# A planned DeltaNet stage: two transposing copies of each block inverse moved to the end of their slot, three large table writes spread over six slots, and one slot more ahead of the weight scales

## The chip, the cores and the metric

The kernel runs on one core of a Trainium2 chip. The metric is the device time of one launch in microseconds (us). TensorE is called PE here, VectorE DVE, ScalarE ACT, GpSimd POOL; SP is the SyncE queue, which in this kernel does nothing but issue DMAs.

## The reference

One encoder layer is computed for two sequences, of 2048 and 1024 tokens, with a model width of 1024. All projections of the normalised input come from one matrix `w_in`; two token mixers run on parts of it, a neighbourhood attention with a relative position bias and a bidirectional gated DeltaNet:

```python
h = _rms_norm(x, norm_g)
proj = jnp.einsum('btd,de->bte', h, w_in)
...
bias = rpb[:, dr_idx[None, None, :, None], dc_idx[:, :, None, :]]
s = jnp.where(col_ok[:, :, None, :], s + bias.astype(jnp.float32), -jnp.inf)
...
a_mat = jnp.where(strict, jnp.einsum('bhnid,bhnjd->bhnij', kb, k) * decay, 0.0) + jnp.eye(CHUNK, dtype=q.dtype)
sol = lax.linalg.triangular_solve(a_mat, rhs, left_side=True, lower=True, unit_diagonal=True)
...
S, o = lax.scan(step, S0, xs)   # one scan per direction over chunks of 64 tokens
```

The two mixers' outputs are gated, projected, merged and put through one more product with a residual. The triangular solve is what the kernel calls an inverse; the masked bias is what its bias table holds.

## The kernel before

**Two stages and an end.** `deltanet()` (from L167) takes the first 1660 us or so: it makes the projections of the input, the DeltaNet operands, the inverses and the scans. From 1668 us on the neighbourhood attention runs (its products are the tile `ppn`), and the branch products, the merge and the output follow.

**The planner.** In `deltanet()` every instruction of every engine and of the SP queue is emitted from one loop, `step_slot()` (L226 to L248), and `Pinned.call` chains each engine's instructions in the order of emission (so every instruction of the trace has the line of that helper, L61). A step is called a slot. The work is written as Python generators; each `yield n` hands back and comes again n slots later. A slot has fixed points, and between them `fill` puts product matmuls on PE until a cost of a quarter, a half, three quarters and the whole of `UNITS` is reached:

```python
            launch()
            advance("S")
            fill(0.25 * UNITS)
            advance("I")
            fill(0.5 * UNITS)
            advance("WH")
            advance("O", MOST)
            fill(0.75 * UNITS)
            ... # what mid() listed, then what end() listed
            advance("F")
            fill(UNITS)
```

S are the scans (PE `pk`, ACT `vn`, DVE `t` and `S`), I the inverses, W and H the weights, the input's rows and side work such as the bias table, O the operands (DVE `P` and `Vt`, the convolution's taps, at 128x512 each), F the decay tables. `launch` opens new generators when their inputs are planned, and issues the loads of the half tiles `hh` and `hl`, the normalised input in two f16 parts, from `hdr` in DRAM. An operand generator goes ahead only while DVE and ACT have been given less than a cost of MOST in the slot. `end(f, ...)` puts a call at the slot's end, with every generator of the slot ahead of it on the engine's queue.

**The filler.** `products()` (L706) multiplies a tile `w` of `w_in` with a half tile: 24 f16 matmuls of 128x256 into the PSUM tile `pp`, which ACT then reads (into `raw`, the convolution's input, or with a tanh into `thz`, the gates), and for the gates `z` DVE multiplies `thz` by `pp` one slot later. Two half banks of a PSUM tile are handed out in turn, so a product begins only when an earlier `pp` has been read. Where the filler has no product whose weights and input are planned, PE gets f32 transposes of a constant called `idle`, up to half of the slot.

**An inverse** (`inverse`, L987). There are twelve, one per head and pair of blocks, never two at once. They work in three buffers that exist once: X, U (in the trace `YT`) and W (`Yo`). In its first slot four DMAs on SP load from `ed` (eight DMAs of the operands' `P` wrote it) two quarters of X and two of U. Two slots later ACT copies U's rows 32 to 63 into X with a transposed reading order, and DVE does the same for rows 96 to 127 (L1002 and L1003, `X<-YT` 32x1024). One slot after that DVE sets X's diagonal (MEMSET X) and POOL clears U (memset YT). A number of slots later the result goes out to `rd` in four DMAs, comes back as `RR` (which takes X's buffer) in the slot after, and two slots later DVE does a STREAM_TRANSPOSE on it.

**The weights** (`weights(k)`, L530, once for each half k of the rows). A weight tile is staged (`wst<-in_w_in`, 256 KB, issued at a slot's end), and DVE reduces it to its largest absolute value per row (`wm<-wst`). When both halves of a group's tiles have been reduced, `factors` (L396) makes the scales: DVE reduces `wm` to `wma`, one slot later PE spreads it over the partitions with transposes `pm`, and DVE reduces `pm` and makes `wsc` and `wfc`. `split_tile` then reads the staged weights again and makes their two f16 parts (`w`).

**The bias table** (`bias_table`, L495) is a side work in the middle of the stage. It fills the DRAM table `ud`, which the attention reads later in 256 loads `bt<-ud`: three large writes of a constant from `ng` over the whole table, one third each, and then 48 small ones `ud<-rp`, two to a slot.

Of the kernel before, what the change touches and what calls it, by code (L numbers as in the profile page):

```python
# [12 lines left out]
AF = mybir.ActivationFunctionType  # L13
# [32 lines left out]
def emit(nc, tc, x_prompt, x_sample, norm_g, w_in, attn_q_norm_g, attn_k_norm_g, attn_rpb, dn_conv_w, dn_a_log,  # L46
# [31 lines left out]
    V, S, G, T, SY = (Pinned(e) for e in (nc.vector, nc.scalar, nc.gpsimd, nc.tensor, nc.sync))  # L78
# [22 lines left out]
    def pow2(m, p, s, k, V=V):  # L101

        V.tensor_scalar_max(m, m, 1e-30)
        V.tensor_scalar(p.bitcast(I32), m.bitcast(I32), 0x7F800000, None, op0=ALU.bitwise_and)
        V.tensor_scalar(s.bitcast(I32), p.bitcast(I32), -1.0, float((254 + k) << 23), op0=MUL, op1=ADD)
# [7 lines left out]
    def allmax(sm, m2, m, ps):  # L113


        n = m.shape[1]
        for a in range(0, n, ps[2]):
            c = min(ps[2], n - a)
            pm = ps[0].tile([128, ps[2], 128], F32, name="pm", tag=ps[1])
            for i in range(c):  # L120
                T.transpose(pm[:, i], m[:, a + i:a + i + 1].to_broadcast([128, 128]), ident)
            V.tensor_reduce(m2[:, a:a + c], pm[:, 0:c], axis=AX.X, op=MAX)
# [44 lines left out]
    def deltanet():  # L167
# [26 lines left out]
        def end(f, *a):  # L194

            ends_.append((f, a))
# [199 lines left out]
        def factors(a, b, ts):  # L396

            n = b - a
            m3 = sm.tile([128, 3, 8], F32, name="wma", bufs=2)
            m, m2, p = (m3[:, i] for i in range(3))  # L400
            V.tensor_reduce(m[:, 0:n], wm2[:, a:b], axis=AX.X, op=MAX)
            yield
            pms = []
            for c in range(0, n, 4):
                pm = ps_tr.tile([128, 4, 128], F32, name="pm", tag="tr")
                for i in range(c, min(c + 4, n)):
                    T.transpose(pm[:, i - c], m[:, i:i + 1].to_broadcast([128, 128]), ident)
                pms.append(pm)
            if prologue:
                yield  # L410
            for c, pm in zip(range(0, n, 4), pms):
                k = min(4, n - c)
                V.tensor_reduce(m2[:, c:c + k], pm[:, 0:k], axis=AX.X, op=MAX)
            pow2(m2[:, 0:n], p[:, 0:n], wsc[:, a:b], 14)
            V.tensor_scalar(wfc[:, a:b], p[:, 0:n], pg, 2.0 ** -24, op0=MUL, op1=MUL)
            for t in ts:
                if t.kind == "z":
                    f = wfc[:, t.n:t.n + 1]
                    V.tensor_copy(zf[:, 4 * t.i + t.h:4 * t.i + t.h + 1], f)
                    if t.i == 0:  # L420
                        V.tensor_tensor(dngz[:, t.h:t.h + 1], dng, f, op=MUL)
# [73 lines left out]
        def bias_table():  # L495


            gq2, gk2 = sm.tile([128, 1], F32, name="gq2", bufs=1), sm.tile([128, 1], F32, name="gk2", bufs=1)
            for j in range(2):
                SY.dma_start(gq2[64 * j:64 * j + 64], attn_q_norm_g[0].rearrange("(p o) -> p o", o=1))  # L500
                SY.dma_start(gk2[64 * j:64 * j + 64], attn_k_norm_g[0].rearrange("(p o) -> p o", o=1))
            rp = wk.tile([120, 64], F32, name="rp", tag="gr", bufs=1)
            rp, ng = rp[:, 0:31], rp[:, 32:64]
            SY.dma_start(rp, attn_rpb[0].rearrange("h r c -> (h r) c"))
            G.memset(ng, NEG)
            yield 2

            V.scalar_tensor_tensor(gg, in0=gq2, scalar=0.125, in1=gk2, op0=MUL, op1=MUL)
            V.scalar_tensor_tensor(gq2, in0=gg, scalar=-1.0, in1=gg, op0=MUL, op1=MAX)
            yield  # L510
            allmax(sm, gk2, gq2, TR)
            V.tensor_scalar_max(gk2, gk2, 2.0 ** -10)
            pow2(gk2, pq, gq2, 0)
            V.tensor_tensor(gg, gg, gq2, op=MUL)
            V.tensor_scalar_mul(npq, pq, -1.0)
            V.tensor_scalar_mul(rp, rp, gq2[:120])
            for ct in range(3):
                SY.dma_start(ud[16 * ct:16 * ct + 16].rearrange("i r k -> r i k"), ng[:, None, :].to_broadcast([120, 16, 32]))
            yield 3
            for ct, off in enumerate((0, -8, -16)):  # L520
                for ci in range(16):
                    w0 = (max(ci - 8, 0), ci, min(8 + ci, 16))[ct]
                    d0 = w0 + off - ci + 15
                    SY.dma_start(ud[16 * ct + ci, :, w0:w0 + 16], rp[:, d0:d0 + 16])
                    if ci % 2:
                        yield
# [3 lines left out]
        def weights(k):  # L530

            def max_(*a):
                yield from maximum(*a, k)
                maxed[k] += 1

            extra = [v[0][:, 256 * i:256 * i + 256] for v in (w_branch_a, w_branch_b) for i in range(4)]
            extra += [w_out[0][:, 128 * i:128 * i + 128] for i in range(8)]
            extra += [win[:, c:c + 128] for c in (QA, KA, VA)]
            extra = list(enumerate(extra, NT + 1))
            for p in range(1, 5):  # L540
                ts = [s[p] for s in streams if len(s) > p]
                for t in ts:
                    yield from max_(win[:, t.c:t.c + 128], t.n)
                if k:
                    while maxed[0] < maxed[1]:
                        yield
                    yield from factors(ts[0].n, ts[-1].n + 1, ts)
                    facs[0] = p
                    yield
                while facs[0] < p:  # L550
                    yield
                for s in streams[:4]:
                    yield from split_tile(s[p], s[p - 1], k)
                if p < 4:
                    for s in streams[4:]:
                        for _ in range(2):
                            if extra:
                                i, src = extra.pop(0)
                                yield from max_(src, i)
                        yield from split_tile(s[p], s[p - 1], k)  # L560
                else:
                    for i, src in extra:
                        yield from max_(src, i)
            if not k:
                return
            while maxed[0] < maxed[1]:
                yield

            m1 = sm.tile([128, 2], F32, name="am1", bufs=1)
            V.tensor_reduce(m1[:, 0:1], wm2[:, NT + 1:NT + 9], axis=AX.XY, op=MAX)  # L570
            V.tensor_reduce(m1[:, 1:2], wm2[:, NT + 9:NT + 17], axis=AX.XY, op=MAX)
            m3 = sm.tile([128, 3], F32, name="am4", bufs=1)
            V.tensor_reduce(m3, wm2[:, NT + 17:NT + 20], axis=AX.X, op=MAX)
            yield
            m2 = sm.tile([128, 2], F32, name="am2", bufs=1)
            allmax(sm, m2, m1, TR)
            pow2(m2, abp[:, 0:2], abp[:, 2:4], 14)
            V.tensor_scalar_mul(so4, so_, 0.25)
            outs.append(1)
            yield  # L580
            m2 = sm.tile([128, 3], F32, name="am3", bufs=1)
            allmax(sm, m2, m3, TR)
            s3 = sm.tile([128, 3], F32, name="as3", bufs=1)
            pow2(m2, abp[:, 4:7], s3, 14)

            for j, c in enumerate((QA, KA, VA)):
                while streams[4 + j][3].left:
                    yield
                wt = wdp.tile([128, 2, 8, 128], F16, name="w")
                sts = [staged(win[:, c:c + 128], i) for i in range(2)]  # L590
                yield 2
                for i, st in enumerate(sts):
                    whl(wt[:, 0, 4 * i:4 * i + 4], wt[:, 1, 4 * i:4 * i + 4], st, s3[:, j:j + 1])
                yield 2
                for a in range(2):
                    SY.dma_start(wt0[:, 1024 * (3 * a + j):1024 * (3 * a + j + 1)], wt[:, a].rearrange("p k c -> p (k c)"))
# [390 lines left out]
        def inverse(h, it):  # L987
# [8 lines left out]
            Xr, Ur = (t[:, 0:1024].rearrange("p (r k) -> p r k", r=32) for t in (X, U))  # L996
# [2 lines left out]
                SY.dma_start(X[q:q + 32, 0:1024], ed[0].rearrange("c b r k -> (c b) (r k)"))  # L999
                SY.dma_start(U[q + 32:q + 64], ed[1].rearrange("c b r k -> (c b) (r k)"))  # L1000
            yield 2
            S.activation(Xr[32:64], Ur[32:64].rearrange("p r k -> p k r"), AF.Copy)  # L1002
            V.tensor_copy(Xr[96:128], Ur[96:128].rearrange("p r k -> p k r"))  # L1003
            yield
            V.memset(X[:, 0:1024:33], 1.0)

# [1049 lines left out]
```

## Time and profile before

| | before |
|---|---|
| device time, median of 3 runs | 2773.81 us |
| lowest and highest of them | 2767.05 and 2774.55 us |
| the profiled execution's own time | 2774.7 us |
| its span, first to last instruction | 2772.9 us |
| mean granted PE clock over the span | 0.993 |
| share of the span that PE is busy | 97% |
| DVE, ACT, POOL | 64%, 50%, 35% |

A row of the timeline gives the start in us, how long the row's instructions took together, the engine, the source line, the operation with what it writes and reads, the shape, how many instructions the row holds and, in brackets, how long the engine was idle before it and what ended that. SPq stands for the SP queue's issues. A stretch of the timeline shows where PE had nothing to do; PEclk is the TensorE clock that was granted in a stretch, 1.00 being full speed.

### The profile page before, as it was taken

How to read it: one execution, taken by the hardware profiler on the slowest of the kernel's cores; microseconds unless marked ns; L12 is line 12 of the kernel's file. 1: busy time of each engine (PE TensorE's matmuls, PEld its weight loads, DVE VectorE, ACT ScalarE, POOL GpSimd, SP SyncE). 2: the span in 40 equal slices, each digit the busy share in tenths (PEclk: the TensorE clock that was granted, in tenths of full speed). 3: DMA queues.
4: the chain of work that ended last, by engine and by line, in shares of the span. 5: the costliest groups of instructions: out<-in, count | busy, mean ns of one | idle time of the engine just before them, and what ended most of it. 6: DMA issues, size and time to landing. Idle time of an engine off the chain costs nothing.

```text
span 2772.9 us, 65318 instructions
## 1 busy us (share of the span) xinstructions
PE 2693.2 (97%) x25080; PEld 2160.1 (78%) x25080; DVE 1763.7 (64%) x4099; ACT 1392.1 (50%) x3861; POOL 962.9 (35%) x1737
## 2 busy tenths in 40 slices
PE   7999999999999999999999999999999999999999
PEld 6888888988889888999888896666666666776675
DVE  6767866576775766747666423666666677556654
ACT  4455564555545655455554534666666764211211
POOL 2233231231222322222322305445444444554453
PEclk9999999999999999999999999999999999999999
DMA  7433442354533444323446648433332565444341
GB/s 244 156 118 92 126 128 85 106 150 112 131 101 104 131 135 127 89 89 108 123 118 179 187 126 222 120 112 89 102 94 86 151 205 200 167 168 158 115 146 69
DMA packets 503974, 365.02 MB, mean 132 GB/s; under 512 B 146035, under 2 KB 452847, under 8 KB 502767
## 3 DMA queue, kind: packets, MB, share of 16 engines
q1 hardware_dynamic: 503663, 360.85, 43.7%
q8 instruction: 198, 3.24, 0.5%
q14 instruction: 113, 0.93, 0.1%
HBM read 262.53 MB, written 98.20 MB: 130 GB/s over the span
## 4 chain that ended last, share of the span: by engine, by line
PE 73%; DVE 11%; DMA 5%; ACT 4%; SPq 3%; issue 2%; POOL 1%; DVEq 0%; POOLq 0%; ACTq 0%
PE pp L61 31%; PE ppn L61 10%; PE pk L61 6%; SPq L61 3%; DVE YT L61 2%; PE pT L61 2%; PE pS L61 2%; PE lv L61 2%; PE pon L61 1%; DVE P L61 1%; DVE Yo L61 1%; PE gq L61 1%; ACT P L61 1%; PE ptk L61 1%; PE idle L61 1%
## 5 line engine op out<-in xcount | busy, mean ns | idle before, releaser
L61 PE MATMUL pp<-hh,w 128*128 128x256 f16 x6912 | 1197.1, 274 | 13.7 <-DVE thz L61 8.4
L61 PEld LDWEIGHTS <-w 128*128 128x128 f16 x10368 | 1013.8, 99 | 146.0 <-issue 13.3
L61 PE MATMUL pp<-hl,w 128*128 128x256 f16 x3456 | 948.4, 274 | 6.1 <-DMA hl<-hdr 3.8
L61 PE MATMUL ppn<-whi,rh 128*128 128x384 f16 x768 | 250.4, 326 | 1.6 <-ACT qs L61 1.6
L61 PEld LDWEIGHTS <-y 128*128 128x128 f16 x2304 | 224.7, 98 | 34.7 <-issue 6.6
L61 PE MATMUL ppn<-whi,rl 128*128 128x384 f16 x768 | 251.3, 327 | 0.0
L61 PE MATMUL ppn<-wlo,rh 128*128 128x384 f16 x768 | 250.4, 326 | 0.0
L61 PEld LDWEIGHTS <-rh 128*128 128x128 f16 x1536 | 144.6, 98 | 71.7 <-issue 1.8
L61 POOL TENSOR_TENSOR th<-th 128x128 f32<-128x128 f32 (+1 forms) x240 | 148.2, 635 | 145.7 <-DVE th L61 132.5
L61 PEld LDWEIGHTS <-mm 128*128 128x128 f16 x1008 | 98.6, 98 | 115.2
L61 ACT ACTIVATE thz<-pp,wfc 128x256 f32<-128x256 f32 x288 | 124.0, 472 | 122.5 <-PE pp L61 92.7
L61 ACT ACTIVATE mm<-th 128x256 f16<-128x256 f32 x144 | 58.9, 445 | 227.9 <-POOL th L61 227.9
L61 DVE TENSOR_TENSOR pl<-pT,ph 128x384 f16<-128x384 f32 (+1 forms) x192 | 110.8, 599 | 82.1 <-ACT ph L61 80.8
L61 POOL TENSOR_TENSOR rqk<-rqk,mhalf 128x4 f32<-128x4 f32 x48 | 51.9, 1081 | 293.7 <-DVE rqk L61 287.3
L61 DVE CUSTOM_DVE_ANT_0 Sb<-pS,bt 128x384 f32<-128x384 f32 (+1 forms) x192 | 108.8, 598 | 67.0 <-DMA vd<-vt 23.5
L61 ACT ACTIVATE vn<-pk,nbeg 128x128 f32<-128x128 f32 x176 | 65.1, 370 | 160.6 <-PE pk L61 160.2
L61 ACT ACTIVATE Sb<-Sb,nm,pq 128x384 f32<-128x384 f32 (+1 forms) x192 | 140.0, 733 | 1.2 <-DVE nm L61 1.1
L61 PEld LDWEIGHTS <-rl 128*128 128x128 f16 x768 | 74.9, 98 | 61.2 <-issue 30.1
L61 ACT ACTIVATE raw<-pp,wfc 128x256 f32<-128x256 f32 x144 | 63.7, 472 | 116.7 <-PE pp L61 113.7
L61 ACT ACTIVATE Os<-pon,rsn 128x64 f32<-128x64 f32 x192 | 49.9, 312 | 142.8 <-PE pon L61 142.7
L61 DVE SCALAR_TENSOR_TENSOR P<-raw,cw,P 128x512 f32<-128x512 f32 x144 | 116.1, 806 | 0.6
L61 DVE SCALAR_TENSOR_TENSOR S<-S,egl,pk 128x128 f32<-128x128 f32 x160 | 54.8, 343 | 91.2 <-PE pk L61 67.1
(621 smaller groups left out, 5653.4 us busy)
## 6 DMA issues: line engine op xcount, KB each, us to landing
wst<-in_w_in SPq DMA_DIRECT2D x124, 256.0 KB
gtd<-thz SPq DMA_DIRECT2D x192, 128.0 KB
hh<-hdr SPq DMA_DIRECT2D x96, 256.0 KB
hl<-hdr SPq DMA_DIRECT2D x96, 256.0 KB
th<-gtd SPq DMA_DIRECT2D x24, 1024.0 KB
vw<-vd SPq DMA_DIRECT2D x320, 64.0 KB
IT<-gd SPq DMA_DIRECT2D x48, 256.0 KB
bt<-ud SPq DMA_DIRECT2D x256, 48.0 KB
```

What stands on the lines that cost most here:

```text
L61: i = f(*a, **k)
```

## The change

Three edits, none of which adds or removes an operation of the computation.

- In `inverse` the two copies `X<-YT` go on the list that is emitted at their slot's end. They stay in the same slot, two after the loads that they read.
- In `bias_table` the `yield` is moved into the loop over the three large writes: one write every two slots in place of three in one slot, so that the small writes begin seven slots after the first large one where it was three.
- In `weights(1)` one more `yield` stands behind the loop that waits until both halves have been reduced, ahead of `factors` (four times) and ahead of the scales of the later weights (once).

```diff
 bias_table():
             for ct in range(3):
                 SY.dma_start(ud[16 * ct:16 * ct + 16].rearrange("i r k -> r i k"), ng[:, None, :].to_broadcast([120, 16, 32]))
-            yield 3
+                yield 2
+            yield
 weights(k):
                     while maxed[0] < maxed[1]:
                         yield
+                    yield
                     yield from factors(ts[0].n, ts[-1].n + 1, ts)
...
             while maxed[0] < maxed[1]:
                 yield
+            yield
 
             m1 = sm.tile([128, 2], F32, name="am1", bufs=1)
 inverse(h, it):
             yield 2
-            S.activation(Xr[32:64], Ur[32:64].rearrange("p r k -> p k r"), AF.Copy)
-            V.tensor_copy(Xr[96:128], Ur[96:128].rearrange("p r k -> p k r"))
+            end(S.activation, Xr[32:64], Ur[32:64].rearrange("p r k -> p k r"), AF.Copy)
+            end(V.tensor_copy, Xr[96:128], Ur[96:128].rearrange("p r k -> p k r"))
             yield
```

The planner decides the order of everything behind an edit anew. The number of instructions of each engine stays as it was, but for 29 `idle` transposes fewer (245 for 274), and the stage has 459 slots where it had 461. Three places follow.

DVE at the first inverse, 206 us in the trace of before, where X<-YT is the copy. Before:

```order
L61 SCALAR_TENSOR_TENSOR thz<-thz,pp 128x256
L61 COPY X<-YT 32x1024
L61 SCALAR_TENSOR_TENSOR xt<-xt,ss,grow 128x1024
L61 SCALAR_TENSOR_TENSOR P<-raw_1831,P 128x512
L61 SCALAR_TENSOR_TENSOR Vt<-raw_1938,cw,Vt 128x512
L61 MEMSET X 128x32
L61 SCALAR_TENSOR_TENSOR P<-raw_2000,cw,P 128x512
L61 TENSOR_TENSOR hl<-pt,hh 128x4x128 x2
```

After:

```order
L61 SCALAR_TENSOR_TENSOR thz<-thz,pp 128x256
L61 SCALAR_TENSOR_TENSOR xt<-xt,ss,grow 128x1024
L61 SCALAR_TENSOR_TENSOR P<-raw_1833,P 128x512
L61 SCALAR_TENSOR_TENSOR Vt<-raw_1940,cw,Vt 128x512
L61 COPY X<-YT 32x1024
L61 MEMSET X 128x32
L61 SCALAR_TENSOR_TENSOR P<-raw_2002,cw,P 128x512
L61 TENSOR_TENSOR hl<-pt,hh 128x4x128 x2
```

The copy has gone behind `xt` (a row of the normalised input), `P` and `Vt`, to the end of its slot, and stands right ahead of the MEMSET of X, which belongs to the next slot.

SP around the read-back of an inverse, 804 to 813 us in the trace of before (`rd` is the inverse's result on its way out, `RR` the read-back of it, `ed` the next operands' way out, `ud` the bias table's small writes). Before:

```order
L61 DMA hl<-hdr_67 128x1024
L61 DMA ud<-rp 120x16 x2
L61 DMA rd_10933<-Yo 512x1x32 x4
L61 DMA ud<-rp 120x16 x2
L61 DMA ed_11595<-P 32x4x32 x8
L61 DMA RR<-rd_10933 128x16x32
L61 DMA ud<-rp 120x16 x2
L61 DMA szd_85<-thz 128x256
```

After:

```order
L61 DMA hl<-hdr_67 128x1024
L61 DMA ud<-rp 120x16 x2
L61 DMA rd_10904<-Yo 512x1x32 x4
L61 DMA ud<-rp 120x16 x2
L61 DMA RR<-rd_10904 128x16x32
L61 DMA ud<-rp 120x16 x2
L61 DMA ed_11614<-P 32x4x32 x8
L61 DMA szd_85<-thz 128x256
```

`RR` has gone ahead of the eight writes of `ed`, which come from an operand generator that is one slot later against the inverse than it was.

DVE at the last of the four groups of scales, 1331 to 1335 us in the trace of before. Before:

```order
L61 COPY ZZ<-lv_19016 128x256
L61 TENSOR_REDUCE wm_141<-wst 128x1 x2
L61 TENSOR_REDUCE wma<-wm_141 128x4
L61 SCALAR_TENSOR_TENSOR Vt<-raw_17975,cw,Vt 128x512
L61 COPY P<-lv_19065 64x4x64 x2
L61 TENSOR_REDUCE wma<-pm 128x4
L61 TENSOR_SCALAR wma<-wma 128x4 x2
L61 TENSOR_SCALAR wsc<-wma 128x4
```

After:

```order
L61 COPY ZZ<-lv_19196 128x256
L61 TENSOR_REDUCE wm_141<-wst 128x1 x2
L61 COPY P<-lv_19239 64x4x64 x2
L61 TENSOR_REDUCE wma<-wm_141 128x4
L61 SCALAR_TENSOR_TENSOR P<-gq,nbeta,IT 128x128 x2
L61 TENSOR_TENSOR IT<-gq,IT 128x2x128
L61 SCALAR_TENSOR_TENSOR P<-gq,nbeta,IT 128x128 x2
L61 TENSOR_TENSOR IT<-gq,IT 128x2x128
L61 TENSOR_REDUCE wma<-pm 128x4
L61 TENSOR_SCALAR wma<-wma 128x4 x2
```

Between the last `wm<-wst` and `wma<-wm` lies a slot's end with two copies of `P` where they followed one another directly, and the transposes `pm` of PE come one slot later again.

## The prediction

> **What bounds the kernel now.** I read the page's busy shares first, then the busy time by stretch:
>
> ```profile
> span 2772.9 us, 65318 instructions
> PE 2693.2 (97%) x25080; PEld 2160.1 (78%) x25080; DVE 1763.7 (64%) x4099; ACT 1392.1 (50%) x3861; POOL 962.9 (35%) x1737
> ```
>
> ```profile
> 0.00:200.00 200.00, 177.84 (x1800) 157.81 (x1801) 139.94 (x286) 98.38 (x214) 53.45 (x111) 0.97 0.53 170
> 200.00:1655.00 1455.00, 1416.73 (x14745) 1259.93 (x14743) 941.39 (x2110) 772.21 (x2280) 375.32 (x719) 0.99 0.43 121
> 1668.00:2773.00 1105.00, 1085.60 (x8423) 729.68 (x8420) 681.47 (x1696) 517.40 (x1357) 531.03 (x905) 1.00 0.44 137
> ```
>
> PE is the bound in every stage. Its number of instructions stays the same but for 29 idle transposes, so only two things can change the time: PE's gaps and the clock at which it runs. Between 200 and 1655 us, where the edits lie, PE is idle for 1455.00 - 1416.73 = 38.3 us: that is the most that gaps can give back there. Behind 1668 us no edit acts except through what the first stage hands over.
>
> Next I read the waits, PE's and DVE's:
>
> ```profile
> PE pp L61 <- DVE thz L61: 8.6, 5, 3.1
> PE ptk L61 <- DVE P L61: 5.0, 4, 3.2
> ```
>
> ```profile
> DVE X L61 <- DMA YT<-ed: 17.2, 9, 4.5
> ```
>
> The two longest kinds of PE waits in this stage that the edits could touch end on DVE, and DVE waits nine times, 17.2 us in all, for the load that the moved copy reads. The timeline has to show in which of the nine PE stood too. It does in three. In the others PE had filler behind it, and nothing is to be had.
>
> Last I read the granted clock behind such gaps:
>
> ```profile
> 210.54:213.95 3.41, 3.41 (x19) 2.43 (x17) 3.31 (x10) 2.24 (x11) 0.84 (x2) 0.50 0.46 184
> 667.92:671.34 3.42, 2.85 (x14) 2.29 (x14) 1.92 (x7) 3.42 (x7) 1.87 (x2) 0.50 0.62 194
> 821.52:824.94 3.42, 3.42 (x29) 2.45 (x29) 2.25 (x6) 0.54 (x2) 0.00 (x0) 0.50 0.30 90
> 1333.52:1336.94 3.42, 3.42 (x19) 2.42 (x18) 3.27 (x10) 0.00 (x0) 0.89 (x3) 0.50 0.83 258
> 1027.31:1030.72 3.41, 3.41 (x32) 3.09 (x32) 2.35 (x6) 2.86 (x7) 2.43 (x3) 1.00 0.57 181
> ```
>
> The column after the engines is PEclk. Four stretches of 3.41 us have half the clock, and each starts at or just before the end of a PE gap told of below; the fifth, behind a gap of 2.40 us, has the whole clock. A stretch at half clock does 1.7 us less of work, so a gap can cost 1.7 us beyond its own length.
>
> **The change part by part.** *The copies.* At the first inverse:
>
> ```profile
> 200.54 0.44 SPq L61 DMA_DIRECT2D YT<-ed  x1
> 205.84 1.06 DVE L61 COPY X<-YT 32x1024 f32<-32x1024 f32 x1 [3.80 <-DMA YT<-ed]
> 208.14 1.64 DVE L61 SCALAR_TENSOR_TENSOR P<-raw,P 128x512 f32<-128x512 f32 x1
> 209.70 1.64 DVE L61 SCALAR_TENSOR_TENSOR Vt<-raw,cw,Vt 128x512 f32<-128x512 f32 x1
> 211.32 0.09 DVE L61 MEMSET X<- 128x32 f32 x1
> 209.92 0.63 PE L61 MATMUL ptk<-ident,P 128*128 128x128 f32 x4 [3.16 <-DVE P L61]
> ```
>
> DVE stands 3.80 us for the load, issued 5.3 us before it lands; behind the copy are `xt` and `P`, and PE's `ptk` needs that `P`. With the copy behind `Vt` the wait and the copy, 3.80 + 1.06 = 4.9 us, leave the path; PE's gap is 3.16, so all of it goes, and with it the window at 210.54: 3.16 + 1.7 = 4.9 us. The new place was reached at 211.3 and would be at about 211.3 - 4.9 = 206.4, 0.6 us behind the landing at 205.8. The cover is thin; if the load came later, the wait would stand before MEMSET and the next slot's `P`, and cost a part of the same 3.8 us.
>
> The same in the second and the third place:
>
> ```profile
> 664.27 1.07 DVE L61 COPY X<-YT 32x1024 f32<-32x1024 f32 x1 [4.54 <-DMA YT<-ed]
> 668.03 0.41 DVE L61 SCALAR_TENSOR_TENSOR thz<-thz,pp 128x256 f32<-128x256 f32 x1
> 668.49 0.37 PE L61 MATMUL pp<-hh,w 128*128 128x256 f16 x1 [3.14 <-DVE thz L61]
> 1023.09 1.06 DVE L61 COPY X<-YT 32x1024 f32<-32x1024 f32 x1 [3.81 <-DMA YT<-ed]
> 1027.31 0.27 PE L61 MATMUL pp<-hh,w 128*128 128x256 f16 x1 [2.40 <-DVE thz L61]
> ```
>
> Here the product's half banks are freed by `thz`, queued behind the copy. Both gaps are shorter than the DVE wait in front of them, so both go: 3.14 + 1.7 = 4.8 and 2.40. Here the copy comes behind a `thz` that needs PE's own product, by which time the load has landed. Sum of the copies: 12.1 us. What is late next in each is the next slot's work, which has the slack of a slot.
>
> *The yield ahead of the scales.* At the last group:
>
> ```profile
> 1331.30 0.69 DVE L61 TENSOR_REDUCE wm<-wst 128x1 f32<-128x512 f32 x1 [2.99 <-DMA wst<-in_w_in]
> 1332.87 0.16 DVE L61 TENSOR_REDUCE wma<-wm 128x4 f32<-128x8 f32 x1
> 1333.17 0.76 PE L61 MATMUL pm<-ident,wma 128*128 128x128 f32 x4 [2.65 <-DVE wma L61]
> 102.29 0.65 PE L61 MATMUL pm<-ident,wma 128*128 128x128 f32 x4 [0.41 <-DVE wma L61]
> 103.57 0.30 PE L61 MATMUL pr<-ident,tmp 128*64 128x128 f32 x1 [0.63 <-DVE wma L61]
> ```
>
> `pm` waits for `wma`, which stands behind two reductions that wait for a late load. A slot more between them (the stage's 1655 us over 461 slots: 3.6 us) covers 2.65 us. DVE still waits for the load, 2.99 us, but what is behind it then is a slot's end. Gain 2.65 + 1.7 = 4.4. At the first group 0.41 + 0.63 = 1.0. The price of the yield is that four groups of weights come one slot later; if the filler had to wait, idle transposes would be added. The new order has fewer of them, 245 for 274, so I take nothing.
>
> *What the yields and the slots move.* One inverse's read-back goes ahead of eight `ed` writes:
>
> ```profile
> 807.77 4.50 SPq L61 DMA_DIRECT2D ed<-P  x8
> 812.32 0.43 SPq L61 DMA_DIRECT2D RR<-rd  x1
> 815.68 0.71 DVE L61 STREAM_TRANSPOSE RR<-RR 128x512 f32<-128x512 f32 x1 [5.08 <-DMA RR<-rd]
> 816.42 2.54 ACT L61 ACTIVATE P<-RR 32x128 f32<-32x128 f32 x8 [2.24 <-DVE RR L61]
> 819.86 0.42 DVE L61 SCALAR_TENSOR_TENSOR thz<-thz,pp 128x256 f32<-128x256 f32 x1 [3.47 <-ACT thz L61]
> 820.59 1.79 PE L61 MATMUL pk<-S,KQ 128*128 128x128 f32 x7 [1.67 <-DVE S L61]
> ```
>
> The chain runs from `RR` over ACT's eight copies, ACT's `thz`, DVE's `thz` and `S` to PE. `RR` issued up to 4.5 us sooner takes away 1.67 + 1.7 = 3.4 us. The reverse happens to another inverse, whose `RR` now stands behind such writes: from 0 to those 3.4 us; I take 1.0, a third, since three inverses stand so in the old order and one of them shows a gap. One `pk` wait later on goes by a new order:
>
> ```profile
> 1483.11 0.75 PE L61 MATMUL pk<-t,P 128*128 128x128 f32 x4 [0.79 <-DVE t L61]
> ```
>
> Such small gaps in the re-dealt slots can be won and lost: +0.8 won, and 2 us (0 to 6) for gaps that I can't foresee.
>
> *The bias table's writes.* They hold the SP queue, and PE doesn't notice:
>
> ```profile
> 725.79 7.60 SPq L61 DMA_DIRECT2D ud<-rp  x3
> ```
>
> ```profile
> 716.00:734.00 18.00, 17.80 (x275) 15.01 (x274) 12.84 (x29) 14.19 (x45) 11.87 (x20) 1.00 0.68 155
> ```
>
> PE is busy for 17.80 of 18 us there. Spread out they hold up other loads less; nothing is to be won: 0. What it could lose, since the small writes now end later, is bounded by the read-back's 3.4; I take 0.
>
> *The end of the stage.* In the new order 28 more PE instructions (20 idle, 8 `ptf`) stand before the last product, and 57 fewer behind it:
>
> ```profile
> 1658.57 9.60 PE L61 MATMUL idle<-ident 128*128 128x128 f32 x84
> ```
>
> At 9.60 / 84 = 0.114 us each the last product comes 3.2 us later than the gaps alone would have it. The attention's first `ppn` waits for loads that follow the last stores, so most of it is passed on; the planner has two slots fewer, which can bring the loads forward by up to 2.8 us. Cost between 0.3 and 4.9 (3.2 and a half-clock window); I take 1.7.
>
> Sum: gains 12.1 + 4.4 + 1.0 + 3.4 + 0.8 = 21.7; costs 1.0 + 2 + 1.7 = 4.7; net 17.0. Against the profiled execution, 2774.7 us, that gives 2757.7, rounded 2758. The median of the runs, 2773.8, lies 0.9 lower and the three runs spread over 7.5 us; I leave the number.
>
> [...] The gap of 1.67 us at 820.59 has a half-clock stretch behind it. [...]
>
> **The rivals.** *Slower: ACT's copy in the scan's way.* ACT's part of the copy takes longer than DVE's and now stands at the slot's end, directly ahead of the next slot's scan, whose `vn` and `thz` PE waits for:
>
> ```profile
> 204.85 2.00 ACT L61 ACTIVATE X<-YT 32x1024 f32<-32x1024 f32 x1 [3.26 <-DMA YT<-ed]
> ```
>
> For it: at 816.42 a burst of 2.54 us on ACT ahead of `thz` ends in PE's gap of 1.67 us and a half-clock stretch, 3.4 us. With 2.00 us at twelve inverses that could be 12 x 3.4 = 41 us. Against it: those eight copies are in all twelve inverses and led to a gap in one, after `RR` was 5.08 us late, and ACT is busy for only 50%. At eight inverses: 27 us, 2757.7 + 27 = 2785. It decides (slower by 0.3%, 8.3 us) from 17 + 8.3 = 25 us, between seven and eight inverses.
>
> *No change: the gaps move.* After the first inverses the order of every slot differs, and the removed gaps at 668, 1027, 820 and 1333 (15.0 us in all) come back at other loads. What then stays is the first inverse and the first group, 4.9 + 1.0, less the end's 1.7 and the 2: 2772. For it: nine waits for `YT` gave three gaps by chance of position. Against it: all twelve copies leave the middle of the slot, so that kind of gap has no place to come back to.
>
> *The read-back keeps its gap.* `RR` is still late by its own load, and the 3.4 stays: 2761.
>
> *Only long gaps cost clock.* If the half-clock stretches at 821 and 1333 are not their gaps' doing, 1.7 + 1.7 stays: 2761. [...]
>
> **How the numbers follow.** Forecast 2758, chance 0.45; the read-back or the clock rival, 2761, 0.2 together; the gaps move, 2772, with cases between it and the forecast, 0.28; slower, 0.07. The forecast's own bounds: all gaps gone and no cost but 0.3 at the end gives 2774.7 - 21.7 + 0.3 = 2753, and a few half-clock stretches elsewhere can fall either way (four of them 7 us): 2746 at the low end. The upper end takes in most of the case of moved gaps: 2771. A measurement tells some 0.3%, 8.3 us, from no change: below 2765.5 is faster. That holds for the first two and a third of the third, 0.45 + 0.2 + 0.09 = 0.74; the rest of the third, 0.19, is the same; 0.07 slower.
>
> **What would show it.** Right: no DVE idle ahead of `X<-YT` that PE shares, no PE gap over 2 us at the first inverses and at `pm`, half-clock windows down from those four, `RR` issued within 2 us of its slot's begin. Wrong: ACT's `X<-YT` directly ahead of a `vn` or `thz` that PE waits for; a new wait of DVE at the slot's end; a later first `ppn` against the last product; as many half-clock stretches as before at other places.

## The result and the profile after

The changed kernel takes 2795.08 us (median of 4 runs, 2794.37 to 2797.28) against 2774.18 us (4 runs, 2767.05 to 2774.66): a ratio of 1.0084, 95% interval 1.007 to 1.0099. It is slower by 21 us, where 16 us less were forecast. The profiled execution took 2794.6 us.

The head of its page:

```profile
span 2792.8 us, 65286 instructions
PE 2695.0 (96%) x25051; PEld 2158.6 (77%) x25051; DVE 1761.1 (63%) x4099; ACT 1395.9 (50%) x3861; POOL 964.2 (35%) x1737
```

PE is busy for 1.8 us more, and the span is 19.9 us longer: 18.1 us are new idle time of PE. The stretch from 200 to 1672 us shows where most of it lies. Its rows, of before and then of after (length, then the busy time of PE, PEld, DVE, ACT and POOL, PEclk, DMA share, GB/s):

```profile
200.00:1672.00 1472.00, 1433.71 (x14885) 1274.88 (x14883) 942.33 (x2119) 776.31 (x2291) 378.37 (x722) 0.99 0.44 123
```

```profile
200.00:1672.00 1472.00, 1420.32 (x14760) 1262.45 (x14758) 947.62 (x2117) 778.68 (x2288) 373.27 (x717) 0.99 0.42 120
```

PE was idle there for 38.3 us and now for 51.7. The gaps that were forecast to go did go, for the most part; others came. First those that went. The timeline of after at the first inverse, DVE's rows and then PE's:

```profile
203.36 1.65 DVE L61 SCALAR_TENSOR_TENSOR Vt<-raw,cw,Vt 128x512 f32<-128x512 f32 x1
205.05 1.06 DVE L61 COPY X<-YT 32x1024 f32<-32x1024 f32 x1
204.69 0.60 PE L61 MATMUL ptk<-ident,P 128*128 128x128 f32 x4
```

The copy waits for nothing at its new place, and `ptk` has no bracket: the gap of 3.16 us is gone. The read-back at the sixth inverse, on SP and DVE of after:

```profile
804.50 0.39 SPq L61 DMA_DIRECT2D RR<-rd  x1
808.42 0.71 DVE L61 STREAM_TRANSPOSE RR<-RR 128x512 f32<-128x512 f32 x1 [2.09 <-DMA RR<-rd]
```

`RR` goes out 1.7 us behind the last `rd` where it was 5.8 us, and no gap of PE follows.

Now what came. Five places of after, rows of the engine that held PE up and PE's own:

```profile
654.70 1.46 ACT L61 ACTIVATE w<-wst,wsc 128x512 f16<-128x512 f32 x2 [4.89 <-DMA wst<-in_w_in]
656.19 1.93 ACT L61 ACTIVATE X<-YT 32x1024 f32<-32x1024 f32 x1
658.66 0.37 ACT L61 ACTIVATE P<-pk,egc 128x128 f32<-128x128 f32 x1
659.08 0.49 PE L61 MATMUL pk<-vn,kh 128*128 128x128 f32 x2 [4.14 <-ACT P L61]
...
968.54 1.48 DVE L61 TENSOR_REDUCE wm<-wst 128x1 f32<-128x512 f32 x2 [5.65 <-DMA wst<-in_w_in]
971.73 0.37 PE L61 MATMUL pp<-hh,w 128*128 128x256 f16 x1 [3.80 <-DVE thz L61]
...
1075.31 1.47 DVE L61 TENSOR_REDUCE wm<-wst 128x1 f32<-128x512 f32 x2 [5.63 <-DMA wst<-in_w_in]
1079.29 1.01 PE L61 MATMUL pk<-S,KQ 128*128 128x128 f32 x3 [3.16 <-DVE S L61]
...
1327.85 0.69 DVE L61 TENSOR_REDUCE wm<-wst 128x1 f32<-128x512 f32 x1 [1.12 <-DMA wst<-in_w_in]
1329.07 0.69 DVE L61 TENSOR_REDUCE wm<-wst 128x1 f32<-128x512 f32 x1 [0.53 <-DMA wst<-in_w_in]
1329.68 1.44 DVE L61 SCALAR_TENSOR_TENSOR P<-raw,P 128x512 f32<-128x512 f32 x1
1331.26 0.63 PE L61 MATMUL ptk<-ident,P 128*128 128x128 f32 x4 [3.34 <-DVE P L61]
...
1555.13 0.61 ACT L61 ACTIVATE wos<-wst,abp 128x384 f16<-128x384 f32 x1 [4.77 <-DMA wst<-in_w_out]
1557.95 1.35 PE L61 MATMUL ptf<-ident,P 128*128 128x128 f32 x4 [3.21 <-ACT P L61]
```

They read alike. A reader of a staged weight (`w`, `wm`, `wos` from `wst`) waits 1 to 6 us for its load; what the kernel has put behind it on the same queue starts after it (on ACT `X<-YT` at 656.19 and `P` at 658.66 us, behind the wait of 4.89 us that ends at 654.70); and a few instructions later stands one that PE needs. With two more of that kind, 2.09 us at 765.36 (behind a wait of `wm` of 3.64 us) and 2.76 us at 1538.53 (behind one of `wos` of 7.01 us), these gaps come to 4.14 + 3.80 + 3.16 + 3.34 + 3.21 + 2.09 + 2.76 = 22.5 us. The waits by kind, before and then after, show the same in sum:

```profile
DVE wm L61 <- DMA wst<-in_w_in: 23.4, 17, 4.5
ACT wos L61 <- DMA wst<-in_w_out: 18.0, 9, 3.6
ACT w L61 <- DMA wst<-in_w_in: 4.9, 3, 3.0
```

```profile
DVE wm L61 <- DMA wst<-in_w_in: 25.4, 19, 5.7
ACT w L61 <- DMA wst<-in_w_in: 17.1, 9, 4.9
ACT wos L61 <- DMA wst<-in_w_out: 16.0, 11, 4.8
DVE wos L61 <- DMA wst<-in_w_out: 12.3, 3, 7.0
DVE wm L61 <- DMA wst<-in_w_out: 6.3, 3, 3.6
```

46.3 us of waits of DVE and ACT for staged loads (47.5 with 1.2 us of `wm` for `in_w_out`) have become 77.1. The granted clock is at half in windows of 3.41 us, and some of the new ones lie at the same places. Three stretches, the second two windows long:

```profile
659.43:662.85 3.42, 3.42 (x19) 2.48 (x18) 2.12 (x6) 2.07 (x5) 2.01 (x2) 0.50 0.67 192
970.05:976.87 6.82, 5.14 (x63) 3.42 (x64) 5.73 (x8) 2.79 (x6) 4.09 (x3) 0.50 0.34 99
1079.27:1082.69 3.42, 3.40 (x26) 2.69 (x27) 1.92 (x5) 0.08 (x1) 0.00 (x0) 0.50 0.81 260
```

The three terms of the prediction's sum account for the later end of the stage to within 1.9 us. Up to the end of its last product PE was idle for 60.4 us before and is for 72.8, the clock was at half for 34.1 us and is for 41.0, and 162 `idle` transposes have become 182. In the half-clock stretch that starts at 1331.86 us two `pp` matmuls take 0.43 us from start to start (1334.19 to 1334.62), just behind it two take 0.22 (1336.05 to 1336.27); so I count half of such a stretch's length as work not done. 12.4 + 6.9 / 2 + 20 x 0.114 = 18.1 us, and the last product comes 16.2 us later.

### The profile page after: what moved, and what is told of

It is laid out like the page before. It is cut to its first block, busy times and chain, and to the rows that moved or that the text cites. A ratio compares the mean times of both kernels' runs of the same rounds, so it can differ in the third digit from the quotient of the medians.

```text
span 2792.8 us, 65286 instructions
## 1 busy us (share of the span) xinstructions
PE 2695.0 (96%) x25051; PEld 2158.6 (77%) x25051; DVE 1761.1 (63%) x4099; ACT 1395.9 (50%) x3861; POOL 964.2 (35%) x1737
## 5 line engine op out<-in xcount | busy, mean ns | idle before, releaser
L61 PE MATMUL pp<-hh,w 128*128 128x256 f16 x6912 | 1195.9, 274 | 12.4 <-DVE thz L61 6.5
L61 ACT ACTIVATE Os<-pon,rsn 128x64 f32<-128x64 f32 x192 | 49.9, 312 | 145.1 <-PE pon L61 144.9
```

The source lines that it names most:

```text
L61: i = f(*a, **k)
```

## The experiments

In the expectations "theory 1" and "theory 2" say that the new yields re-deal the slots and that the loss lies there; the main rival says that ACT's copy at the slot's end stands in the scan's way. Each ratio is to the kernel before, run beside it on the same chip; the times are medians, so a difference of two times need not match the ratio to the last 2 us. A trace shows one execution, and single executions of one kernel differ by up to some 15 us (those with the late readers lie between 2781.36 and 2796.87).

**The three parts apart.** Each kernel holds one or two of the edits of the diff shown above and nothing else.

*The copies alone:*

```diff
-            S.activation(Xr[32:64], Ur[32:64].rearrange("p r k -> p k r"), AF.Copy)
+            end(S.activation, Xr[32:64], Ur[32:64].rearrange("p r k -> p k r"), AF.Copy)
-            V.tensor_copy(Xr[96:128], Ur[96:128].rearrange("p r k -> p k r"))
+            end(V.tensor_copy, Xr[96:128], Ur[96:128].rearrange("p r k -> p k r"))
```

> Only the two copies X<-YT go to the slot's end; the order of the rest stays nearly as before. Theory 1 (the new yields re-deal the slots, and loads of staged weights then come late in other places; the copies themselves do what was forecast): the gaps of 3.16, 3.14 and 2.40 us at the three inverses and two half-clock stretches go, about 12 us, so 2760 to 2765 us. Rival (ACT's copy of 2.0 us at the slot's end stands in the scan's way, as at the gap of 4.14 us at 659 us in the changed kernel): 2775 us or more, with new PE gaps released by ACT or by a DVE step behind ACT, right behind the inverses' copies.

Measured: 2768.13 us, ratio 0.9976 (0.9965 to 0.9988): 8 us gained on 2776.24 by the medians, 6.7 by the ratio. That lies in neither expectation's range, but nearer to theory 1's. No PE gap of over 1.2 us stands at the three inverses, and DVE's 17.2 us of waits for `YT` are gone altogether. Up to the last product PE is idle for 51.7 us in place of 60.4: the 8.7 us of the three gaps, to the tenth. The two half-clock windows at 210 and 668 us are gone too, but others came, and the time at half clock is the same 34.1 us.

*The bias table's writes alone:*

```diff
-            yield 3
+                yield 2
+            yield
```

> Only the three large writes of the bias table are spread. Both theories: no PE gap stands there, so 2774 us within 4 us. A third theory (the small writes, now later, block the SP queue ahead of other loads) would have 2780 or more.

Measured: 2776.59 us, ratio 1.0005 (0.9995 to 1.0016): no change.

*The yields alone,* here ahead of `factors`, and once ahead of `m1`:

```diff
                     while maxed[0] < maxed[1]:
                         yield
+                    yield
                     yield from factors(ts[0].n, ts[-1].n + 1, ts)
```

> Only the five new yields ahead of the weight scales. Theory 1: the loss is here; without the copies' gain the three gaps at the inverses may come back on top, so 2790 to 2808 us, with PE gaps of 3 to 4 us behind DVE's wm<-wst waiting for its load. Rival (ACT's copy costs it): the gap at pm goes and nothing else changes for the worse, 2765 to 2776 us.

Measured: 2784.89 us, ratio 1.004 (1.0026 to 1.0054). The yields alone lose, with no copy moved, so ACT's copy can't be the whole of the loss. But theory 1's 2790 to 2808 us failed as well: this is about half of what the changed kernel loses. The largest of its gaps behind the start, on DVE and PE:

```profile
969.95 1.45 DVE L61 TENSOR_REDUCE wm<-wst 128x1 f32<-128x512 f32 x2 [5.32 <-DMA wst<-in_w_in]
972.15 1.09 PE L61 MATMUL ptk<-ident,P 128*128 128x128 f32 x4 [5.09 <-DVE P L61]
```

*The copies and the bias table's writes, no yields:*

> The copies and the bias table's writes without the yields. Theory 1: as with the copies alone, 2758 to 2766 us. Rival: as the changed kernel or little better, 2780 us or more.

Measured: 2762.48 us, ratio 0.9958 (0.9942 to 0.9974). Theory 1's range held; this kernel is faster than the one before and the changed one. Its row of the same stretch:

```profile
200.00:1672.00 1472.00, 1443.75 (x14938) 1280.70 (x14937) 951.18 (x2125) 783.75 (x2309) 392.82 (x748) 1.00 0.45 125
```

PE is idle for 28.3 us, 10 less than before and 23 less than in the changed kernel. The writes alone were worth nothing, and the intervals of this ratio and of the copies alone meet; whether the writes add to the copies is left open. The two traces speak against it: up to the last product PE is idle for 49.9 us here and for 51.7 with the copies alone, and what sets them apart is the clock, at half for 13.7 us here and for 34.1 there. This trace is of an execution of 2755.8 us, some 7 below the kernel's median, so the 23 us may overstate the difference.

**Which yield.** The copies and the writes stay in, and the yield is taken group by group. The yield ahead of `m1` is in only with `p != 2`:

```diff
+                    if p == 4:   # or p == 1, p == 2, p != 2
+                        yield
                     yield from factors(ts[0].n, ts[-1].n + 1, ts)
```

*At the last group only:*

> The copies, the bias table's writes and the yield at the last group of scales only, where the order of everything else is held but for that group's few instructions. Measured without the yield: 2762.5 us, with a gap of 2.03 us at pm. Theory 1 (a yield is cheap where it re-deals nothing): that gap and perhaps a half-clock stretch go, 2757 to 2762 us. Rival (the yield itself costs, by weights that come a slot later): 2764 us or more.

Measured: 2762.42 us, ratio 0.9959 (0.9945 to 0.9973). Between the two expectations: it costs nothing and gains nothing. The gap at `pm`, 2.03 us without the yield, is gone, but 2.53 us have come at a product that waits for its `hl`, at the same place of the stage. First the row without the yield, then the rows with it:

```profile
1315.05 0.66 PE L61 MATMUL pm<-ident,wma 128*128 128x128 f32 x2 [2.03 <-DVE wma L61]
```

```profile
1323.58 1.49 DVE L61 TENSOR_REDUCE wm<-wst 128x1 f32<-128x512 f32 x2 [3.50 <-DMA wst<-in_w_in]
1325.36 0.27 PE L61 MATMUL pp<-hl,w 128*128 128x256 f16 x1 [2.53 <-DMA hl<-hdr]
```

*At the first group only:*

> The copies, the bias table's writes and the yield at the first group only. It shifts the stream of weights by one slot against all the rest from slot 17 on, and the order differs nearly everywhere. Theory 1 (the loss comes of the new meeting of the staged loads with the other loads): most of the loss is here, 2775 to 2800 us. Rival (each of the five yields costs a share): 2763 to 2770 us, a quarter of the loss or less.

Measured: 2763.59 us, ratio 0.9963 (0.995 to 0.9977). My theory's expectation of 2775 to 2800 failed: this yield changes the order of many rows and costs nothing. The planner's output fits with it afterwards: the scans, inverses and, but for two steps, the operands stay in the same slots, 461 in all, and the products change places.

*At the second group only:*

> The copies, the bias table's writes and the yield at the second group only. The planner's output with it alone has 459 slots and puts the operands and the inverses from the second group on in the same slots as the changed kernel but for one; with the yields at the first or at the last group alone it has 461, and these measured 2763.6 and 2762.4 us. Theory 2 (the one slot at the second group re-deals the rest of the stage, and the loss is there): 2788 to 2798 us. Rival (the loss needs several yields): 2762 to 2775 us.

Measured: 2792.62 us, ratio 1.0072 (1.0056 to 1.0088): the whole loss but for what the intervals leave, from one yield. Idle time 51.4 us in its row:

```profile
200.00:1672.00 1472.00, 1420.57 (x14765) 1261.77 (x14763) 944.02 (x2117) 777.64 (x2288) 374.82 (x718) 0.99 0.43 120
```

*At all places but the second group:*

> All three edits but without the yield at the second group; the stage has 460 slots. Theory 2: 2757 to 2770 us, like the copies and the bias table's writes without yields (2762.5). Rival (the third group's yield, which re-deals what is behind it, costs as well): 2778 us or more.

Measured: 2780.29 us, ratio 1.0027 (1.0015 to 1.004), idle time 45.2 us. Theory 2 was too narrow. The yields at the first and the last group cost nothing alone; so the third group's, with which the planner has 460 slots and other places for the operands and inverses behind it, is left for most of what this kernel loses against the one without yields (1.0027 against 0.9958). That is by elimination: no run has the third group's yield alone. The planner's output bears it out. With that yield alone it gives the same 460 slots, with every scan and inverse where this kernel has it, and the yield ahead of `m1` alone moves no scan, inverse or operand.

```profile
200.00:1672.00 1472.00, 1426.84 (x14834) 1268.87 (x14832) 947.04 (x2116) 777.92 (x2288) 381.26 (x719) 0.99 0.43 122
```

*Two yields at the second group,* to see another order of the same 459 slots:

```diff
+                    for _ in range(2 * (p == 2)):
+                        yield
                     yield from factors(ts[0].n, ts[-1].n + 1, ts)
```

> As the run with the yield at the second group only (2792.6 us), but two yields there; again 459 slots, in part with other operand and inverse slots. If any re-deal into 459 slots costs, since the same work lies in fewer slots with less slack: 2786 to 2800 us. If the one yield's order is an unlucky one among many: any other place, and 2780 us or less is as likely as not.

Measured: 2793.68 us, ratio 1.0072 (1.0053 to 1.0092). Another order, in part other gaps, the same loss; so it isn't one unlucky meeting. The gap at 1331 us of the changed kernel is there too:

```profile
1332.50 0.64 PE L61 MATMUL ptk<-ident,P 128*128 128x128 f32 x4 [3.99 <-DVE P L61]
```

**The copies in the new order.** The planner lets an operand generator go ahead by what DVE and ACT have been given in the slot. A copy at the slot's end is not counted yet at that point, so the copies' move re-deals the slots as well. One kernel has all three edits and the old charge, one the new order with the copies at their old place:

```diff
+            V.cost += 1124
+            S.cost += 1124
+            end(copies)        # all edits, the charge where it was
...
             S.activation(Xr[32:64], Ur[32:64].rearrange("p r k -> p k r"), AF.Copy)
             V.tensor_copy(Xr[96:128], Ur[96:128].rearrange("p r k -> p k r"))
+            V.cost -= 1124     # the changed kernel's order, the copies not moved
+            S.cost -= 1124
```

> All three edits, but the two copies are charged to the planner where they stood before, so that the operands go ahead in the same slots as with the yields alone. With the yields alone 2784.9 us were measured. Theory 1a (in the changed kernel the copies cost because their lower charge re-dealt the slots once more): the copies gain here as they did alone, about 8 to 12 us, so 2770 to 2778 us. Rival (in this order the copies' place at the slot's end itself costs, ACT and DVE standing at them ahead of the scans): 2786 us or more, as the changed kernel.

Measured: 2784.14 us, ratio 1.0039 (1.0027 to 1.0051), the same as the yields alone, whose 459 slots it has with every scan, inverse and operand in its place. Neither expectation held: in this order the copies' move is worth nothing, and what the changed kernel loses beyond it (1.0084 against 1.0039, the intervals apart) comes of the lower charge.

> The changed kernel's order, with the two copies left at their old place in the middle of the slot but not charged to the planner there, so that all else stays where the changed kernel has it (2795.1 us). If the copies' place at the slot's end is what costs in this order (ACT's copy in the gap at 659 us, DVE's in those at 765 and 1022 us): 2780 to 2790 us. If the order costs and the copies' place still gains: 2797 to 2806 us. Theory 2 with the copies worth nothing in this order, as the run with the old charge had it: 2792 to 2797 us.

Measured: 2800.45 us, ratio 1.0097 (1.008 to 1.0114). That is in the second expectation's range, where the order costs and the copies' place still gains. But against the changed kernel's 1.0084 the intervals meet, so a gain isn't shown; the rival is out, since with the copies at their old place the kernel is no faster. PE's rows show both sides of it:

```profile
205.41 0.63 PE L61 MATMUL ptk<-ident,P 128*128 128x128 f32 x4 [2.34 <-DVE P L61]
659.11 0.49 PE L61 MATMUL pk<-vn,kh 128*128 128x128 f32 x2 [1.66 <-ACT P L61]
1025.55 0.71 PE L61 MATMUL pk<-S,KQ 128*128 128x128 f32 x4 [3.85 <-DVE S L61]
```

At 659 us the gap is 1.66 us in place of 4.14: there ACT's copy, 1.93 us long, did stand in the scan's way, and the gap is 2.5 us shorter without it. But the first inverse's gap is back with 2.34, and the one at 1022 us, 1.87 us in the changed kernel, is 3.85.

**The staged loads.** In the changed kernel, the readers moved to their slot's end (with the planner's charge kept), the loads moved from the slot's end to the generator's place, ahead of the operands' DMAs, and both:

```diff
-            S.activation(t.w_[:, 0, ks], st, AF.Identity, scale=s)
+            end(lambda: S.activation(t.w_[:, 0, ks], st, AF.Identity, scale=s))
-            amax(wm2[:, n, k:k + 1], st)
+            end(amax, wm2[:, n, k:k + 1], st)
...
-            end(SY.dma_start, st, src[...])
+            SY.dma_start(st, src[...])     # from slot 40 on
```

> The changed kernel with the two first readers of each staged weight load (DVE's wm and ACT's w) at their slot's end too, charged where they stood; PE's order is held. Theory 1 (the staged loads come late and their readers hold the queues): the gaps at 659, 765, 972, 1079 and 1331 us, 16.5 us in all, and three or four half-clock stretches go or shrink, so 2770 to 2780 us. Rival (the loss lies in the order itself and in the scans' and operands' own waits): 2790 us or more, with gaps of the same length released by other things.

Measured: 2791.03 us, ratio 1.006 (1.0043 to 1.0076). By its time that is the rival's case, and the interval meets the changed kernel's (1.007 to 1.0099). The trace is of an execution of 2781.4 us, 10 below the median. In it, of the five gaps those at 765 and 1331 us are gone and three are shorter, 5.3 us in place of 16.5 in all:

```profile
660.45 0.49 PE L61 MATMUL pk<-vn,kh 128*128 128x128 f32 x2 [1.31 <-ACT P L61]
971.11 0.27 PE L61 MATMUL pp<-hh,w 128*128 128x256 f16 x1 [2.43 <-DVE thz L61]
1074.14 0.71 PE L61 MATMUL pk<-S,KQ 128*128 128x128 f32 x4 [1.52 <-DVE S L61]
```

The mechanism is shown for these gaps. But little of it reached the time: other gaps came, such as 3.75 us at 611 us, where a product waits for its `hl`, and up to the last product PE's idle time fell only from 72.8 to 68.7 us. The rest of what this trace is shorter by is the clock, at half for 17.1 us in place of 41.0.

> The changed kernel with the staged weights' loads (from slot 40 on) issued where their generator asks for them, ahead of the operands' loads and stores of the same slot, and not at the slot's end. If the late landing of these loads is what holds the readers and PE (22.5 us of gaps in the changed kernel's trace at 659, 765, 972, 1079, 1331, 1538 and 1558 us): half of that or more goes, 2775 to 2787 us. Rival (the loads are late because the DMA queues are full whatever the order, or other loads come late in their place): 2790 us or more.

Measured: 2793.28 us, ratio 1.0055 (1.0034 to 1.0075). The median is the rival's case, and again the interval meets the changed kernel's. The gaps at 659 and 972 us fell below 1 us, the one at 1331 stayed; a new one is 3.02 us long:

```profile
720.69 0.44 PE L61 MATMUL pm<-ident,gq 128*128 128x128 f32 x1 [3.02 <-DVE gq L61]
1333.16 0.63 PE L61 MATMUL ptk<-ident,P 128*128 128x128 f32 x4 [3.23 <-DVE P L61]
```

> The changed kernel (2795.1 us) with the staged loads issued early in their slot and their first readers at the slot's end, both together; PE's order is held. If late staged loads are the whole of the loss behind the second group: 2765 to 2775 us. If they are about a third of it, as each remedy alone suggests, and the rest is made of the scans', operands' and inverses' own waits in the new slots: 2782 to 2790 us.

Measured: 2784.69 us, ratio 1.004 (1.0027 to 1.0053), as expected for "a part", and clear of the changed kernel's interval. Of the five gaps four are gone and the one at 1079 us is 1.75 us. The waits of DVE and ACT for staged loads are now below those of before, 12.3 + 14.3 + 8.5 + 5.1 + 2.1 = 42.3 us:

```profile
ACT wos L61 <- DMA wst<-in_w_out: 14.3, 11, 4.5
DVE wm L61 <- DMA wst<-in_w_in: 12.3, 7, 5.0
DVE wos L61 <- DMA wst<-in_w_out: 8.5, 2, 7.3
ACT w L61 <- DMA wst<-in_w_in: 5.1, 5, 1.6
DVE wm L61 <- DMA wst<-in_w_out: 2.1, 1, 2.1
```

The loss against the kernel without yields is 1.0084 - 0.9958 = 0.0126; both remedies give back 0.0044 of it, a third; between the two traces about half of that is idle time of PE up to the last product (72.8 and 66.2 us) and half the clock (41.0 and 27.3 us at half). What is left stands at other waits, the longest this one, where DVE waits 8.25 us for a small load that the bias table's generator issues:

```profile
720.88 0.16 DVE L61 SCALAR_TENSOR_TENSOR gg<-gq,gk 128x1 f32<-128x1 f32 x1 [8.25 <-DMA gk<-in_attn_k_norm_g]
721.44 0.45 PE L61 MATMUL pm<-ident,gq 128*128 128x128 f32 x1 [5.24 <-DVE gq L61]
```

*The early loads in the good order* (copies and writes, no yields):

> The copies and the bias table's writes without yields (2762.5 us), with the staged loads issued early in their slot. If late staged loads cost in this order too (gaps of 2.03 us at pm and some of 1 us at w): 2756 to 2761 us. If these loads, issued early, push others back: 2763 to 2772 us.

Measured: 2765.17 us, ratio 0.9976 (0.9964 to 0.9987), against 0.9958 without (the intervals meet): no gain. The trace has a new gap of 2.45 us at 971 us, at a product that waits for its `hl`, which fits with the early loads taking the place of others; that they do so throughout isn't shown.

## Why the prediction was wrong

Point by point, by its own steps.

- *The copies.* Right in mechanism, too large by the clock. Alone they gained 7 to 8 us of the 12.1 worked out: the gaps' 8.7 us went, and the 3.4 us for two half-clock windows did not come, since as many windows came elsewhere. The thin cover at the first inverse held: no wait at the new place. In the re-dealt order the move was worth nothing.
- *The yield ahead of the scales.* Here a step failed: "DVE still waits for the load, 2.99 us, but what is behind it then is a slot's end". The yield moved `pm` out from behind the wait, and the wait stayed on DVE's queue. In the changed kernel the next in line was an operand's `P`, and PE lost 3.34 us at `ptk` where it had lost 2.65 at `pm`. With the yield at the last group alone another gap came at the same place of the stage, at a product that waits for its `hl`, and the 4.4 us came to nothing.
- *The read-back.* Right: issued 1.7 us behind the last `rd`, and the gap of 1.67 us gone.
- *The bias table's writes.* Right: nothing.
- *The end of the stage.* The 20 `idle` transposes came, at 2.3 us. But the last product came 16.2 us later than before (1670.5 for 1654.3 us at its start), by far the most of it through the gaps and half-clock windows told of above. PE's rows from there on:

```profile
1670.65 7.26 PE L61 MATMUL idle<-ident 128*128 128x128 f32 x65
1679.08 0.32 PE L61 MATMUL ppn<-whi,rh 128*128 128x384 f16 x1 [1.17 <-DMA whi<-wt]
```

  The first `ppn` comes 8.4 us behind the start of the idle transposes, where before it came 13.6 us behind; gaps of 5.0 us at it and the next few, 1.17 of them ahead of it, take most of that back. The passage itself cost about nothing. That the loads could come forward by up to 2.8 us, as the low end of this cost has it, is a figure that no row gives; the 5.1 us here are what came of it.
- *The new order.* This is the step that decided: "2 us (0 to 6) for gaps that I can't foresee", and for the four groups of weights that come a slot later "the new order has fewer of them [idle transposes], 245 for 274, so I take nothing". I had counted what the planner counts, and put the rest at 2 us. The planner's own cost of PE improved by two slots. On the chip PE stood idle for 12.4 us more than before up to the last product, although the gaps that were aimed at were gone, and for 22.9 us more than in the kernel without the yields (72.8 for 49.9); the time at half clock, 41.0 us for 13.7 there, costs, at half of its length, (41.0 - 13.7) / 2 = 13.7 us on top of these 22.9. These are waits that the planner doesn't price: how long a load takes, and which reader stands ahead of whom on a queue.
- *The clock.* Each of the four half-clock stretches was read as starting at or just before the end of a gap. Three start 0.35 to 0.93 us behind it: at 210.54, 821.52 and 1333.52 us, for gaps that end at 209.92, 820.59 and 1333.17. The 1.7 us for a window, half of its 3.41, fits with the pace of the `pp` matmuls above, 0.43 us in it for 0.22 behind it; the sum for the later end is too coarse to tell, 18.1 us with it and 14.7 without for the 16.2 measured. Which gap brings a window could not be read from these rows, as the last section has it.
- *The rivals.* That the gaps move was the right kind of thing, but its price was bounded by the gaps that had been removed, and nothing bounds it so: between 650 and 1600 us the changed kernel has seven gaps of over 2 us, 22.5 us in all, where before had four with 10.2. ACT's copy cost some 2.5 us at one inverse and not 3.4 at eight.

What is shown: the loss comes with the yields at the second group, by a run of its own, and at the third, by elimination, which put the operands and inverses into other slots; a third of it goes with the two remedies for late staged loads. Split by edits, the 0.0126 are 0.0042 that the copies and writes bring without the yields and not with them, 0.0040 that the yields lose alone and 0.0045 that the copies' lower charge adds. What stays open is the rest of the mechanism: why these orders wait longer. The number of slots doesn't settle it. Two orders with 459 slots cost 1.0072 each and the changed kernel's 1.0084, but the yields alone and the kernel with the old charge have 459 slots too and cost 1.0040 and 1.0039, and one with 460 cost 1.0027, where the copies' kernels with 461 ran at 0.996 to 0.998. That the same work in fewer slots leaves each queue less slack may be a part of it, but no run here changed the slack alone.

## What to carry to other kernels

An edit that makes a planner deal the work anew is a new kernel behind that point: its price is the re-deal's, and the gaps that it was meant to remove say little of it. Try the edits apart, those that hold the order first; here the ones that held it were worth 0.4%, and one `yield` more took back nearly three times that. A wait that is moved behind one reader on a queue whose order the kernel fixes is still on that queue: look up what will be next in line. Here it was an operand's `P`, and PE lost 3.34 us where it had lost 2.65.

## What the runs showed of the hardware

**Which gaps had a half-clock stretch.** Between 100 and 1600 us the traces of before and after have 18 gaps of PE of over 1.6 us and 14 stretches at half clock (PEclk 0.50). Each of the 14 starts at one of these gaps, from 1.68 us ahead of the gap's end to 1.74 us behind it. Behind the four gaps without one the 3.41 us from the gap's end ran at 1.00:

| trace | gap of PE, us | ends at | half-clock stretch starts at | its length, us |
|---|---|---|---|---|
| before | 3.30 | 617.28 | 616.72 | 3.41 |
| before | 3.16 | 209.92 | 210.54 | 3.41 |
| before | 3.14 | 668.49 | 667.92 | 3.41 |
| before | 2.65 | 1333.17 | 1333.52 | 3.41 |
| before | 2.40 | 1027.31 | none | |
| before | 2.05 | 1536.76 | 1538.32 | 3.41 |
| before | 1.81 | 270.24 | 271.98 | 3.41 |
| before | 1.67 | 820.59 | 821.52 | 3.41 |
| after | 4.14 | 659.08 | 659.43 | 3.41 |
| after | 3.80 | 971.73 | 970.05 | 6.83 |
| after | 3.34 | 1331.26 | 1331.86 | 3.41 |
| after | 3.21 | 1557.95 | 1557.14 | 6.83 |
| after | 3.16 | 1079.29 | 1079.27 | 3.41 |
| after | 2.76 | 1538.53 | 1540.07 | 3.41 |
| after | 2.09 | 765.36 | none | |
| after | 1.87 | 1022.33 | none | |
| after | 1.81 | 263.29 | 263.49 | 3.41 |
| after | 1.65 | 1406.62 | none | |

A gap of 1.67 us had one and a gap of 2.40 us had none, so in these rows the length of a gap alone does not tell whether a stretch follows. What decides is not shown: no run changes a gap's length or its place alone. The prediction took the two stretches at 210 and 668 us as won with their gaps; with the copies alone both were gone, and the time at half clock was the same 34.1 us.

**Time and clock.** Over the 191 executions on record of the kernels here, set against the mean of their own kernel, the time falls by 2.3 us for each 0.001 of mean granted clock (correlation -0.77).
